# Layer 1's input projection: the second parts of two column tiles in one run, and two moved steps

## The chip, the cores and the metric

One core of a Trainium2 chip runs the whole kernel. The metric is the device time of one execution in microseconds; the median of three runs is taken. TensorE (PE) multiplies, VectorE (DVE) and ScalarE (ACT) work element by element, GpSimd (POOL) adds a few tiles and issues small DMAs, and SyncE (SP) issues the loads of weights.

## The reference, cut

Two layers over 256 tokens of width 2048, all in float32. Layer 1, the one that is changed, is a Mamba-2 layer:

```python
proj = x @ w_in
z, xbc, dt = jnp.split(proj, [SSD_D_INNER, SSD_D_INNER + SSD_CONV_DIM], -1)
xbc = jax.nn.silu(causal_depthwise_conv(xbc, conv_w, conv_b))
xs, bm, cm = jnp.split(xbc, [SSD_D_INNER, SSD_D_INNER + SSD_N_GROUPS * SSD_D_STATE], -1)
...
y = ssd_chunked(xs, dt, a, bm, cm, chunk)
y = y + d_skip.reshape(g, r)[..., None] * xs
yg = (y * jax.nn.silu(z.astype(jnp.float32))).reshape(b, L, g, SSD_NORM_GROUP)
yg = yg * lax.rsqrt(jnp.mean(yg * yg, -1, keepdims=True) + RMS_EPS)
yg = yg.reshape(b, L, SSD_D_INNER) * norm_g
return yg.astype(x.dtype) @ w_out
```

Layer 2 is sparse attention over the same tokens; the change does not touch it.

## The kernel before

**Split products.** A float32 product is made of three products of rounded parts: every operand is split into a first part, hi, and a second part, lo, and hi x hi + hi x lo + lo x hi are added up in PSUM. xT holds the hi and lo of x side by side, 512 columns per row tile. So with the weights' hi as the stationary operand, one matmul of 512 columns (L327) does hi x hi and hi x lo, and with the weights' lo one matmul of 256 columns (L324) does the third product.

**Units and the stream.** All weights go through one stream of units of 128 x 1024 elements (the class `Stream`). A unit is loaded by SP (L93) into one of four raw buffers, ScalarE copies it rounded into hi (L109), and VectorE subtracts to get lo (L138); hi and lo have four buffers each. `run` (L152) goes from unit to unit: it first has the units up to `i + SPLIT` (four) converted, then writes TensorE's matmuls of unit i, and then takes each side step under way one step on. That gives every engine its order; there is no scheduler, each engine works through its own list and waits by semaphores.

**The projection.** Layer 1's input projection has 160 units, numbered 0 to 159: 8 groups of 20, each group 10 column tiles of two units (one tile B, one C, four x, four z). `stream_w` (L306) writes a unit. For a column tile the order is hi of the first unit, lo of the first, lo of the second, hi of the second: a run of 16 lo matmuls, and, with the next tile's first unit, a run of 16 hi.

**Side steps.** When a column tile is finished, a generator (`conv_steps`, `z_steps`) evacuates it and works on it, a bit per unit. More generators start at unit numbers given by hand in the loop over groups (u = 20 g): `cb_steps` (the products of B and C, after unit u + 9), `xst_steps` (four transposes, the "turned rows" pxs, for the halves of a group, after u + 13 and u + 18), `m_steps` (the masks E and M), `y_steps` (after u + 23 and u + 33), which ends six units on with a matmul ms (L481) that sums the squares, and `norm_steps` for each two groups. A norm begins 40 units after the second group's start, waits for its small DMAs through POOL's queue, and then takes one tile in two units, eight tiles in all: VectorE multiplies (L516, into yf), ScalarE copies hi of yg, VectorE subtracts for its lo (L509). The output projection (`out_proj`, units 160 to 287) reads yg: units 160 to 171 read yg's first 24 tiles, two each.

Of the kernel before, what the change touches and what calls it, by code (L numbers as in the profile page):

```python
# [16 lines left out]
P = 128  # L17
T = 256
D = 2048
KT = D // P  # L20
NG = 8
# [27 lines left out]
SPLIT = 4  # L49
# [10 lines left out]
MOVING, FIRST8, OTHERS = range(3)  # L60


class Unit:


    def __init__(self, src, width, pe, use):
        self.src, self.width, self.pe, self.use = src, width, pe, use


class Stream:  # L70
# [7 lines left out]
        self.limit = 1 << 30  # L78
        self.homes = {}

    def add(self, src, width, pe, use):
        self.units.append(Unit(src, width, pe, use))
        return len(self.units) - 1

    def side(self, i, gen, behind=False):
# [66 lines left out]
    def run(self, end):  # L152
        while self.pos < end:
            i = self.pos
            self.convert_to(i + SPLIT)
            self.units[i].pe(*self.parts.pop(i))
            for behind, (fn, *a) in self.starts.pop(i, []):
                (self.behind if behind else self.active).append(fn(*a))
            self.active = [g for g in self.active if next(g, self) is not self]
            self.behind = [g for g in self.behind if next(g, self) is not self]  # L160
            self.pos += 1
# [9 lines left out]
def trunk_kernel(ctx: ExitStack, tc: tile.TileContext, x, xt, w1, wdt, dtp, prm, wo1,  # L171
                 wkv, wcq, wix, wg, wab, wo2, lnr, out):
    nc = tc.nc
# [12 lines left out]
    st = Stream(nc, wraw, whi, wlo)  # L186
    v = nc.vector

    def acc_tile(name):
        return p_acc.tile([P, 512], F32, tag="acc", name=name)  # L190
# [11 lines left out]
    xT = big.tile([P, KT, 2 * T], F32R, tag="A", name="xT")  # L202
# [20 lines left out]
    def rsqrt(pool, dst, val, n, w, tag):  # L223

        t = pool.tile([n, w], F32, tag=tag, name=tag)
        v.tensor_scalar(dst.bitcast(I32), val.bitcast(I32), -0.5, MAGIC, op0=ALU.mult,
                        op1=ALU.add)
        for k in range(3):
            v.tensor_mul(t, dst, dst)
            v.scalar_tensor_tensor(t, t, -0.5, val, op0=ALU.mult, op1=ALU.mult)  # L230
            v.scalar_tensor_tensor(dst, t, 1.5, dst, op0=ALU.add, op1=ALU.mult)
# [78 lines left out]
    def stream_w(half, cell, name, turn=True):  # L310


        def pe(h, l):
            if half == 0:
                cell["ps"] = acc_tile(name)
            ps, xs = cell["ps"], cell["x"][0]
            first, second = (1, 0) if half and turn else (0, 1)
            for lo in (first, second):
                for k in (0, 1, 6, 7, 4, 5, 2, 3) if lo and half == 0 else range(8):
                    kt, w = half * 8 + k, slice(k * P, (k + 1) * P)  # L320
                    last = half == 1 and lo == second and k == 7
                    if lo:
                        lw = l[:, w] if half else l[:, k // 2, k % 2 * P:(k % 2 + 1) * P]
                        nc.tensor.matmul(ps[:, 0:T], lw, xs[:, kt, 0:T], start=False,  # L324
                                         stop=last, skip_group_check=True)
                    else:
                        nc.tensor.matmul(ps, h[:, w], xs[:, kt, :], start=(kt == 0), stop=last,  # L327
                                         skip_group_check=True)
        return pe

    def halves(dst, ps, wait=True):
# [152 lines left out]
    def norm_steps(b):  # L484

        ms = sp1.tile([2, T], F32, tag="ms", name=f"msv{b}")
        nc.scalar.activation(ms, MS[b][0:2, 0:T], AF.Copy)
        md, rd = (dram.tile([2, T], F32, tag=t, name=f"{t}{b}") for t in ("ms_d", "rs_d"))
        nc.gpsimd.dma_start(md, ms)
        col = sp1.tile([P, 4], F32, tag="col", name=f"col{b}")  # L490
        rcl = sp1.tile([P, 4], F32, tag="rcl", name=f"rcl{b}")
        nc.gpsimd.dma_start(col, md.rearrange("g (q j) -> (g q) j", j=4))
        yield
        yield
        yield
        v.tensor_scalar_add(col, col, 4.0 * RMS_EPS)
        rsqrt(sp1, rcl, col, P, 4, "rq")
        nc.gpsimd.dma_start(rd.rearrange("g (q j) -> (g q) j", j=4), rcl)
        rb = sp1.tile([P, 2, T], F32, tag="rb", name=f"rbs{b}")
        nc.gpsimd.dma_start(rb, rd.rearrange("(o g) t -> o g t", o=1).broadcast_to([P, 2, T]))  # L500
        yield
        yield
        yield
        fts = {}
        for c in range(10):
            if c > 1:
                cc = 8 * b + c - 2
                dst = yg[cc // 16][:, cc % 16, :]
                v.tensor_sub(dst[:, T:2 * T], fts.pop(c - 2), dst[:, 0:T].bitcast(F32))  # L509
            if 0 < c < 9:  # L510
                cc = 8 * b + c - 1
                nc.scalar.activation(yg[cc // 16][:, cc % 16, 0:T], fts[c - 1], AF.Copy)
            if c < 8:
                g, cc = 2 * b + c // 4, 8 * b + c
                ft = fts[c] = sp3.tile([P, T], F32, tag="yf", name=f"yf{cc}")
                v.scalar_tensor_tensor(ft, G[g].pop(("x", c % 4)),  # L516
                                       par[:, PC_NORM + cc:PC_NORM + cc + 1],
                                       rb[:, c // 4, :], op0=ALU.mult, op1=ALU.mult)
            yield
            if b < 3:  # L520
                yield

    xcell = [xT]
    for g in range(NG):
        for kind, n in (("B", 1), ("C", 1), ("x", 4), ("z", 4)):
            for ci in range(n):
                cell = {"x": xcell}
                for half in range(2):
                    k = len(st.units)
                    i = st.add(w1[k], 1024, stream_w(half, cell, f"acc{k}", turn=k > 1),  # L530
                               OTHERS if half else FIRST8)
                if kind == "z":
                    st.side(i, (z_steps, g, ci, cell))
                else:
                    cc = {"x": g * 4 + ci, "B": 32 + g, "C": 40 + g}[kind]
                    st.side(i, (conv_steps, g, kind, ci, cc, cell))
# [67 lines left out]
    for g in range(NG):  # L604
        u = 20 * g
        gap = 5 if g < 7 else 2
        st.side(u + 9, (cb_steps, g))
        st.side(u + 13, (xst_steps, g, 0))
        st.side(u + 18 + (g == NG - 1), (xst_steps, g, 1))
        for c in range(4):  # L610
            st.side(max(u + 5 + gap * c, 9 + c), (abc_steps, g, c))
            st.side(u + 13 + gap * c, (m_steps, g, c))
            if c % 2:
                st.side(u + 18 + max(gap * c, 2 * c), (y_steps, g, c // 2))
        if g % 2:
            st.side(u + 18 + gap * 3 + 7, (norm_steps, g // 2), behind=g < NG - 1)
# [33 lines left out]
    for kt in range(KT):  # L650

        for h in range(2):
            nc.tensor.matmul(p_dt[h * NH1:(h + 1) * NH1, 0:P], w_dt[:, kt, :],
                             xr[:, kt, h * P:(h + 1) * P], start=(kt == 0),
                             stop=(kt == KT - 1), skip_group_check=True)
# [75 lines left out]
    def add_gate(h):  # L731
        cell = {"x": xcell}
        for half in range(2):
            i = st.add(wg[h * 2 + half], 1024, stream_w(half, cell, f"g{h}"),
                       OTHERS if half else FIRST8)
        st.side(i, (gate_steps, h, cell))
# [58 lines left out]
    for kb in range(8):  # L795
        i = st.add(wcq[kb], 1024, stream_tok(kb, 512, cells["q"], "qp",
                                             held if kb < EARLY else None), MOVING)
    st.side(i, (lat_norm, cells["q"], 512, PC_QG, 4, "q", "cqT"))
    for kb in range(8):
        i = st.add(wkv[kb], 672, stream_tok(kb, 336, cells["kv"], "kvp"), MOVING)  # L800
# [7 lines left out]
    def idx_pe(q, cell):  # L808
        def pe(h, l):
            cell["ps"] = acc_tile(f"ix{q}")  # L810
            for k in range(2):
                ps = cell["ps"][:, k * T:(k + 1) * T]
                for kt in range(4):
                    o = (k * 4 + kt) * P
                    nc.tensor.matmul(ps, h[:, o:o + P], cqT[:, kt, 0:T], start=(kt == 0), stop=False)
                    nc.tensor.matmul(ps, h[:, o:o + P], cqT[:, kt, T:2 * T], start=False, stop=False)
                    nc.tensor.matmul(ps, l[:, o:o + P], cqT[:, kt, 0:T], start=False, stop=(kt == 3))
        return pe
# [41 lines left out]
    for q in range(4):  # L860
        cell = {}
        i = st.add(wix[q], 1024, idx_pe(q, cell), MOVING)
# [130 lines left out]
    for p in range(NH2 // 2):  # L993
        src = wab[2 * p]
        i = st.add(wab[2 * p], 1024, pair_a(p), MOVING)
        st.side(i, (evac_steps, p, ("k", "v")))
        i = st.add(wab[2 * p + 1], 1024, pair_b(p), MOVING)
# [348 lines left out]
```

## Time and profile before

| | us |
|---|---|
| median of 3 runs (1230.06 to 1230.5) | 1230.15 |
| the profiled execution, its own time | 1230.57 |
| its span from first to last instruction | 1228.7 |
| TensorE busy in the span | 1223.0 |
| VectorE busy | 936.0 |
| ScalarE busy | 701.9 |
| end of layer 1's input projection (start of the output projection's first matmul, from the span's start) | 491.38 |

The span is what the trace covers; the time of an execution has a little more around it. TensorE's busy time counts matmuls that overlap in the engine's pipeline, so a full row there says only that it had work at hand; how fast it went is read from the distance of starts.

### The profile page before, as it was taken

The numbers are of one execution on the slowest core, as the hardware profiler recorded it, in microseconds if no ns is written. First come the engines' busy times: TensorE is split into PE (matmuls) and PEld (weight loads), VectorE is DVE, ScalarE is ACT, GpSimd is POOL, SyncE is SP. The second block draws the span as 40 slices with busy tenths as digits, with TensorE's granted clock in tenths as the row PEclk, the third lists the DMA queues.
The fourth block names the chain that finished last, engine by engine and source line by source line (L and its number), as shares of the span: only waits on it lengthen the run. The fifth ranks groups of instructions, "written<-read, shape, count | busy, mean of one in ns | idle before, by whom it ended". The sixth has DMA issues, their size and how long they took to land.

```text
span 1228.7 us, 19505 instructions
## 1 busy us (share of the span) xinstructions
PE 1223.0 (100%) x7197; PEld 1064.0 (87%) x7197; DVE 936.0 (76%) x1757; ACT 701.9 (57%) x1274; POOL 65.5 (5%) x102
## 2 busy tenths in 40 slices
PE   9999999999999999999999999999999999999998
PEld 8888888888888888788888898999999999888886
DVE  6978788988898889756557778877777777667457
ACT  6666566666666666544336655566766666433441
POOL 0001011001100110110000000000000000000000
PEclk9999999999999999999999999999999999999999
DMA  8765667566666665676666564454444445875652
GB/s 296 211 196 180 207 185 215 171 208 187 203 185 206 187 205 180 192 236 220 197 194 201 193 212 148 168 170 165 159 154 149 161 155 190 308 230 186 200 196 94
DMA packets 65359, 236.55 MB, mean 193 GB/s; under 512 B 8025, under 2 KB 8161, under 8 KB 64881
## 3 DMA queue, kind: packets, MB, share of 16 engines
q1 hardware_dynamic: 60352, 215.29, 54.2%
q0 software_dynamic: 4912, 20.02, 5.3%
q8 instruction: 57, 0.93, 0.3%
q14 instruction: 38, 0.30, 0.1%
HBM read 231.00 MB, written 4.28 MB: 191 GB/s over the span
## 4 chain that ended last, share of the span: by engine, by line
PE 99%; DMA 1%; SPq 0%; DVE 0%; ACT 0%; DVEq 0%; issue 0%
PE acc L327 24%; PE acc L324 12%; PE g L327 10%; PE o L555 9%; PE o L557 9%; PE o L556 9%; PE g L324 5%; PE y L452 2%; PE q L901 1%; PE q L900 1%; PE q L902 1%; PE pt L963 1%; PE pxs L432 1%; PE k L878 1%; PE k L879 1%; PE k L880 1%
## 5 line engine op out<-in xcount | busy, mean ns | idle before, releaser
L138 DVE TENSOR_TENSOR lo<-raw,hi 128x1024 fp32r<-128x1024 f32 (+1 forms) x404 | 489.0, 1214 | 240.2 <-ACT hi L109 239.8
L109 ACT ACTIVATE hi<-raw 128x1024 fp32r<-128x1024 f32 (+2 forms) x405 | 422.0, 1048 | 214.2 <-PE o L557 160.2
L327 PE MATMUL acc<-xT,hi 128*128 128x512 f32 x1280 | 314.5, 394 | 0.3 <-ACT hi L109 0.3
L327 PEld LDWEIGHTS acc<-xT,hi 128*128 128x128 f32 x1280 | 232.6, 188 | 46.3 <-ACT E L407 1.2
L324 PEld LDWEIGHTS acc<-xT,lo 128*128 128x128 f32 x1280 | 159.4, 188 | 6.4
L324 PE MATMUL acc<-xT,lo 128*128 128x256 f32 x1280 | 161.9, 278 | 0.0
L327 PE MATMUL g<-x1T,hi 128*128 128x512 f32 x512 | 127.4, 395 | 0.0
L327 PEld LDWEIGHTS g<-x1T,hi 128*128 128x128 f32 x512 | 92.4, 188 | 17.5
L555 PE MATMUL o<-hi,yg 128*128 128x512 f32 x256 | 100.3, 392 | 0.0
L557 PE MATMUL o<-hi,yg 128*128 128x512 f32 x256 | 99.7, 389 | 0.0
L556 PE MATMUL o<-lo,yg 128*128 128x512 f32 x256 | 99.6, 389 | 0.0
L555 PE MATMUL o<-hi,og 128*128 128x512 f32 (+1 forms) x256 | 99.6, 389 | 0.0
L557 PE MATMUL o<-hi,og 128*128 128x512 f32 (+1 forms) x256 | 98.9, 386 | 0.0
L556 PE MATMUL o<-lo,og 128*128 128x512 f32 (+1 forms) x256 | 98.8, 386 | 0.0
L354 DVE SCALAR_TENSOR_TENSOR ca<-cr,par,ca 128x255 f32<-128x255 f32 x144 | 69.2, 481 | 3.4
L324 PE MATMUL g<-x1T,lo 128*128 128x256 f32 x512 | 69.3, 280 | 0.0
L324 PEld LDWEIGHTS g<-x1T,lo 128*128 128x128 f32 x512 | 65.8, 188 | 2.9
L357 ACT ACTIVATE cr<-ca 128x256 f32<-128x256 f32 x48 | 20.1, 418 | 77.9 <-DVE ca L354 77.9
L555 PEld LDWEIGHTS o<-hi,yg 128*128 128x128 f32 x256 | 48.1, 188 | 10.1 <-issue 0.2
L557 PEld LDWEIGHTS o<-hi,yg 128*128 128x128 f32 x256 | 48.0, 188 | 10.1
L557 PEld LDWEIGHTS o<-hi,og 128*128 128x128 f32 x256 | 48.1, 188 | 9.9
L556 PEld LDWEIGHTS o<-lo,yg 128*128 128x128 f32 x256 | 48.1, 188 | 9.9
(274 smaller groups left out, 1781.8 us busy)
## 6 DMA issues: line engine op xcount, KB each, us to landing
raw<-in_w_dram SPq DMA_DIRECT2D x160, 512.0 KB, 4.2
raw<-in_wo_dram SPq DMA_DIRECT2D x128, 512.0 KB, 4.2
raw<-in_wg_dram SPq DMA_DIRECT2D x64, 512.0 KB, 3.2
raw<-in_wab_dram SPq DMA_DIRECT2D x32, 512.0 KB, 3.2
abc<-acs_d POOLq DMA_DIRECT2D x32, 256.0 KB, 4.2
raw<-in_wcq_dram SPq DMA_DIRECT2D x8, 512.0 KB, 4.4
raw<-in_wkv_dram SPq DMA_DIRECT2D x8, 336.0 KB, 2.9
scr<-in_xt_dram SPq DMA_DIRECT2D x4, 512.0 KB, 6.5
```

The source lines that it names most:

```text
L109: self.nc.scalar.activation(h[:, cs], r[:, cs], AF.Copy)
L138: eng.tensor_sub(*self.halfway.pop(i))
L324: nc.tensor.matmul(ps[:, 0:T], lw, xs[:, kt, 0:T], start=False, stop=last, skip_group_check=True)
L327: nc.tensor.matmul(ps, h[:, w], xs[:, kt, :], start=(kt == 0), stop=last, skip_group_check=True)
L354: v.scalar_tensor_tensor(acc[:, d:], rw[:, :T - d], w(k), acc[:, d:], op0=ALU.mult, op1=ALU.add)
L357: nc.scalar.activation(rw, acc, AF.Tanh)
L432: nc.tensor.transpose(pm[:, o:o + P], G[g][("x", 2 * half + c)][:, s * P:(s + 1) * P], ident)
L452: nc.tensor.matmul(py[ks, c * T + s * P:(c + 1) * T], xsT[:, s, c, ks], ms[c][k][:, ws], start=(c == 0 and s == 0), stop=(s == 1), skip_gr ...
L555: nc.tensor.matmul(ps, ah, hs, start=(kk == 2 * first), stop=False)
L556: nc.tensor.matmul(ps, ah, ls, start=False, stop=False)
L557: nc.tensor.matmul(ps, al, hs, start=False, stop=(kk == 31))
L878: nc.tensor.matmul(ps, h[:, o:o + P], ckvT[:, ct, 0:T], start=(ct == 0), stop=False)
```

## The change

Of the 160 units, those with `k % 20` up to 15, without the first four, are now taken in fours, that is, two column tiles a and b at a time, by a new function `stream_two`. Its order is: hi of a (two units), the first single hi matmul of b, lo of a (two units), lo of b (two units), and the rest of b's hi. The lo of a pair's first unit is thus used while the second unit is written, and `run` converts one unit less ahead at that step (`kept`). The last four units of a group, and the first four of all, keep the old order.

In `norm_steps` of the first three norms, a pause after the fourth of eight tiles moves the last four tiles five units later (four in the third norm). And `xst_steps` of a group's second half starts after u + 19 in all groups, not u + 18; the ms matmul of the group before stands after the same unit.

```diff
@@ -152,7 +153,7 @@
-            self.convert_to(i + SPLIT)
+            self.convert_to(i + SPLIT - (i > 0 and self.units[i - 1].kept))
@@ -328,6 +329,45 @@
+    def stream_two(j, a, b, name):
+        def hi(cell, half, h, ks):
+            for k in ks:
+                kt = half * 8 + k
+                nc.tensor.matmul(cell["ps"], h[:, k * P:(k + 1) * P], cell["x"][0][:, kt, :],
+                                 start=(kt == 0), stop=(cell is b and kt == 15),
+                                 skip_group_check=True)
+
+        def lo(cell, half, l):
+            for k in range(8) if len(l.shape) == 2 else (0, 1, 6, 7, 4, 5, 2, 3):
+                kt = half * 8 + k
+                lw = (l[:, k * P:(k + 1) * P] if len(l.shape) == 2 else
+                      l[:, k // 2, k % 2 * P:(k % 2 + 1) * P])
+                nc.tensor.matmul(cell["ps"][:, 0:T], lw, cell["x"][0][:, kt, 0:T], start=False,
+                                 stop=(cell is a and kt == 15), skip_group_check=True)
+
+        def pe(h, l):
+            after = st.parts.get(st.pos + 1)
+            if j == 0:
+                a["ps"] = acc_tile(name)
+                hi(a, 0, h, range(8))
+                a["lo"] = l
+            elif j == 1:
+                hi(a, 1, h, range(8))
+                b["ps"] = acc_tile(name + "b")
+                hi(b, 0, after[0], range(1))
+                lo(a, 0, a.pop("lo"))
+                lo(a, 1, l)
+            elif j == 2:
+                lo(b, 0, l)
+                lo(b, 1, after[1])
+                hi(b, 0, h, range(1, 8))
+            else:
+                hi(b, 1, h, range(8))
+        return pe
+
@@ -518,17 +558,26 @@
             if b < 3:
-                yield
+                for _ in range((6, 6, 5)[b] if c == 3 else 1):
+                    yield
...
+                if len(st.units) % 4 == 0:
+                    pair = [{"x": xcell} for _ in range(2)]
                 for half in range(2):
                     k = len(st.units)
-                    i = st.add(w1[k], 1024, stream_w(half, cell, f"acc{k}", turn=k > 1),
-                               OTHERS if half else FIRST8)
+                    if k < 4 or k % 20 > 15:
+                        i = st.add(w1[k], 1024, stream_w(half, cell, f"acc{k}", turn=k > 1),
+                                   OTHERS if half else FIRST8)
+                    else:
+                        cell = pair[k % 4 // 2]
+                        i = st.add(w1[k], 1024, stream_two(k % 4, *pair, f"acc{k}"),
+                                   OTHERS if k % 4 else FIRST8, kept=k % 4 == 0)
@@ -606,7 +655,7 @@
-        st.side(u + 18 + (g == NG - 1), (xst_steps, g, 1))
+        st.side(u + 19, (xst_steps, g, 1))
```

What this does to the orders of the engines is shown at four places. In the names, the number before the underscore counts units for hi, lo and raw, and tiles elsewhere; the one behind it counts buffers.

TensorE, units 68 to 71 (a pair, with the products cb of group 3), before:

```order
L327 MATMUL acc68_2409<-xT_86,hi68_2307 128x512 x8
L324 MATMUL acc68_2409<-xT_86,lo68_2308 128x256 x8
L324 MATMUL acc68_2409<-xT_86,lo69_2345 128x256 x8
L327 MATMUL acc68_2409<-xT_86,hi69_2344 128x512 x8
L381 MATMUL cb3_2470<-C3_2426,B3_2367 128x256
L382 MATMUL cb3_2470<-C3_2426,B3_2367 128x128
L327 MATMUL acc70_2479<-xT_86,hi70_2376 128x512 x8
L324 MATMUL acc70_2479<-xT_86,lo70_2377 128x256 x8
L324 MATMUL acc70_2479<-xT_86,lo71_2404 128x256 x8
L327 MATMUL acc70_2479<-xT_86,hi71_2403 128x512 x8
```

The same units on TensorE now:

```order
L339 MATMUL acc68_2409<-xT_86,hi68_2340 128x512 x8
L339 MATMUL acc68_2409<-xT_86,hi69_2346 128x512 x8
L339 MATMUL acc69b_2441<-xT_86,hi70_2384 128x512
L348 MATMUL acc68_2409<-xT_86,lo68_2341 128x256 x8
L348 MATMUL acc68_2409<-xT_86,lo69_2347 128x256 x8
L421 MATMUL cb3_2466<-C3_2418,B3_2375 128x256
L422 MATMUL cb3_2466<-C3_2418,B3_2375 128x128
L348 MATMUL acc69b_2441<-xT_86,lo70_2385 128x256 x8
L348 MATMUL acc69b_2441<-xT_86,lo71_2404 128x256 x8
L339 MATMUL acc69b_2441<-xT_86,hi70_2384 128x512 x7
L339 MATMUL acc69b_2441<-xT_86,hi71_2403 128x512 x8
```

The two runs of 16 lo matmuls are one of 32, and cb has moved from between hi matmuls into the middle of it.

TensorE, units 78 to 80 (the last tile of group 3 and the next group's first unit; pxs3_1 are the turned rows, ms1 the squares), before:

```order
L324 MATMUL acc78_2763<-xT_86,lo78_2662 128x256 x8
L432 MATMUL pxs3_1_2783<-ident_90,xs3_2_2644 128x128 x2
L432 MATMUL pxs3_1_2783<-ident_90,xs3_3_2721 128x128 x2
L324 MATMUL acc78_2763<-xT_86,lo79_2699 128x256 x8
L327 MATMUL acc78_2763<-xT_86,hi79_2698 128x512 x8
L481 MATMUL ms1_2820<-sq2_3_2687,sel_99 128x256
L327 MATMUL acc80_2835<-xT_86,hi80_2731 128x512 x8
```

The same units on TensorE now:

```order
L325 MATMUL acc78_2755<-xT_86,lo78_2666 128x256 x8
L325 MATMUL acc78_2755<-xT_86,lo79_2695 128x256 x8
L328 MATMUL acc78_2755<-xT_86,hi79_2694 128x512 x8
L521 MATMUL ms1_2802<-sq2_3_2683,sel_99 128x256
L472 MATMUL pxs3_1_2811<-ident_90,xs3_2_2652 128x128 x2
L472 MATMUL pxs3_1_2811<-ident_90,xs3_3_2717 128x128 x2
L339 MATMUL acc80_2826<-xT_86,hi80_2723 128x512 x8
```

The transposes stand behind ms, and no longer inside the lo run.

VectorE, around the steps of units 64 to 66 (xs2 is y's evacuation, M are masks, B3 is group 3's B), before:

```order
L459 SCALAR_TENSOR_TENSOR xs2_1_1879<-xs2_1_1879,par_88,y2_0_2244 128x256
L461 TENSOR_TENSOR xs2_1_1879<-xs2_1_1879,zs2_1_2001 128x256
L138 TENSOR_TENSOR lo68_2308<-raw68_2170,hi68_2307 128x4x256
L420 TENSOR_TENSOR M20_2335<-E20_2253,cbm2_1825 128x384
L420 TENSOR_TENSOR M21_2337<-E21_2256,cbm2_1825 128x384
L138 TENSOR_TENSOR lo69_2345<-raw69_2197,hi69_2344 128x1024
L363 SCALAR_TENSOR_TENSOR B3_2367<-cr35_2191,ca35_2190 128x256
```

The same place on VectorE now:

```order
L499 SCALAR_TENSOR_TENSOR xs2_1_1871<-xs2_1_1871,par_88,y2_0_2244 128x256
L501 TENSOR_TENSOR xs2_1_1871<-xs2_1_1871,zs2_1_2001 128x256
L460 TENSOR_TENSOR M20_2331<-E20_2253,cbm2_1833 128x384
L460 TENSOR_TENSOR M21_2333<-E21_2256,cbm2_1833 128x384
L139 TENSOR_TENSOR lo68_2341<-raw68_2193,hi68_2340 128x4x256
L139 TENSOR_TENSOR lo69_2347<-raw69_2199,hi69_2346 128x1024
L403 SCALAR_TENSOR_TENSOR B3_2375<-cr35_2187,ca35_2186 128x256
```

The conversion of a pair's first unit stands a step later, with that of the second. From B3 on to C3, the other operand of cb, VectorE's rows are the same in both.

VectorE, where the third norm ends (yf22 and yf23 are its last two tiles), before:

```order
L509 TENSOR_TENSOR yg1_563<-yf22_5532,yg1_563 128x256
L138 TENSOR_TENSOR lo166_5668<-raw166_5538,hi166_5667 128x1024
L138 TENSOR_TENSOR lo167_5687<-raw167_5582,hi167_5686 128x1024
L509 TENSOR_TENSOR yg1_563<-yf23_5614,yg1_563 128x256
L138 TENSOR_TENSOR lo168_5715<-raw168_5620,hi168_5714 128x1024
```

And now:

```order
L549 TENSOR_TENSOR yg1_563<-yf22_5659,yg1_563 128x256
L139 TENSOR_TENSOR lo170_5758<-raw170_5665,hi170_5757 128x1024
L139 TENSOR_TENSOR lo171_5778<-raw171_5684,hi171_5777 128x1024
L549 TENSOR_TENSOR yg1_563<-yf23_5709,yg1_563 128x256
L139 TENSOR_TENSOR lo172_5797<-raw172_5715,hi172_5796 128x1024
```

Both tiles stand four conversions later.

## Rows read from the trace of the kernel before

**Rows 1.** The page's chain that ended last, by engine.

```profile
PE 99%; DMA 1%; SPq 0%; DVE 0%; ACT 0%; DVEq 0%; issue 0%
```

**Rows 2.** Waits of TensorE, whole run: engine, line, for whom; us, times, longest.

```profile
PE p_dt L631 <- DVE scr L628: 1.3, 1, 1.3
PE acc L327 <- ACT hi L109: 0.3, 1, 0.3
```

**Rows 3.** Timeline of TensorE: start us, us to last end, operation, shapes, number.

```profile
222.06 2.00 PE L324 MATMUL acc<-xT,lo 128*128 128x256 f32 x16
223.90 3.81 PE L327 MATMUL acc<-xT,hi 128*128 128x512 f32 x16
227.55 2.00 PE L324 MATMUL acc<-xT,lo 128*128 128x256 f32 x16
```

**Rows 4.** The same runs, from windows that begin at their second parts.

```profile
222.99 1.07 PE L324 MATMUL acc<-xT,lo 128*128 128x256 f32 x8
...
225.51 2.20 PE L327 MATMUL acc<-xT,hi 128*128 128x512 f32 x9
```

**Rows 5.** TensorE in the output projection: window, us, busy (number), clock, DMA.

```profile
563.33:576.93 13.60, 13.60 (x61) 1.00 0.58 167
```

**Rows 6.** Timeline of TensorE: pxs in a lo run, ms in a hi run.

```profile
426.70 1.09 PE L324 MATMUL acc<-xT,lo 128*128 128x256 f32 x8
427.64 0.60 PE L432 MATMUL pxs<-ident,xs 128*128 128x128 f32 x4
...
428.99 2.00 PE L327 MATMUL acc<-xT,hi 128*128 128x512 f32 x8
430.83 0.59 PE L481 MATMUL ms<-sq,sel 128*128 128x256 f32 x2
...
433.12 2.01 PE L324 MATMUL acc<-xT,lo 128*128 128x256 f32 x16
```

**Rows 7.** Timeline of TensorE, group 7's end: ms and pxs together.

```profile
488.75 2.00 PE L327 MATMUL acc<-xT,hi 128*128 128x512 f32 x8
...
491.02 0.60 PE L432 MATMUL pxs<-ident,xs 128*128 128x128 f32 x4
491.38 0.47 PE L555 MATMUL o<-hi,yg 128*128 128x512 f32 x1
...
494.00 0.39 PE L557 MATMUL o<-hi,yg 128*128 128x512 f32 x1
```

**Rows 8.** Timeline of TensorE: cb, then y with pxs, between hi matmuls.

```profile
398.37 2.00 PE L327 MATMUL acc<-xT,hi 128*128 128x512 f32 x8
...
402.70 0.63 PE L324 MATMUL acc<-xT,lo 128*128 128x256 f32 x4
...
410.02 2.00 PE L327 MATMUL acc<-xT,hi 128*128 128x512 f32 x8
411.96 1.52 PE L452 MATMUL y<-M,xsT 128*64 128x256 f32 x16
...
415.73 0.52 PE L324 MATMUL acc<-xT,lo 128*128 128x256 f32 x3
```

**Rows 9.** Timelines of VectorE and TensorE: a tile's last writer and its reader.

```profile
217.36 0.42 DVE L363 SCALAR_TENSOR_TENSOR C<-cr,ca 128x256 f32<-128x256 f32 x1
...
219.57 0.59 PE L381 MATMUL cb<-C,B 128*128 128x256 f32 x2
...
243.57 1.22 DVE L138 TENSOR_TENSOR lo<-raw,hi 128x1024 fp32r<-128x1024 f32 x1
...
247.35 1.05 PE L324 MATMUL acc<-xT,lo 128*128 128x256 f32 x7
...
276.76 1.22 DVE L138 TENSOR_TENSOR lo<-raw,hi 128x1024 fp32r<-128x1024 f32 x1 [0.79 <-ACT hi L109]
...
282.28 2.00 PE L324 MATMUL acc<-xT,lo 128*128 128x256 f32 x16
```

**Rows 10.** VectorE: a 40 us window over all engines; its timeline in the output projection.

```profile
200.00:240.00 40.00, 40.00 (x245) 34.04 (x245) 36.95 (x78) 26.03 (x51) 4.33 (x7) 1.00 0.63 196
...
512.46 1.23 DVE L138 TENSOR_TENSOR lo<-raw,hi 128x1024 fp32r<-128x1024 f32 x1 [1.39 <-ACT hi L109]
```

More of the change, by code (lines that the diff above doesn't have):

```diff
@@ L63, with __init__ @@
 class Unit:
-    def __init__(self, src, width, pe, use):
-        self.src, self.width, self.pe, self.use = src, width, pe, use
+    def __init__(self, src, width, pe, use, kept):
+        self.src, self.width, self.pe, self.use, self.kept = src, width, pe, use, kept
 class Stream:
@@ L79, in __init__, with add @@
         self.homes = {}
-    def add(self, src, width, pe, use):
-        self.units.append(Unit(src, width, pe, use))
+    def add(self, src, width, pe, use, kept=False):
+        self.units.append(Unit(src, width, pe, use, kept))
         return len(self.units) - 1
@@ L520, in norm_steps @@
             if b < 3:
-                yield
-    xcell = [xT]
+                for _ in range((6, 6, 5)[b] if c == 3 else 1):
+                    yield
+    xcell, pair = [xT], None
     for g in range(NG):
```

## The prediction, made before the changed kernel was run

> **What bounds the kernel now.** I read the chain that ended last first: 99% of it is TensorE [rows 1]. Then TensorE's waits over the whole run: two, of 1.3 and 0.3 us [rows 2]. So through layer 1's input projection (160 units of weights, up to about 491 us) TensorE hardly ever waits; whatever changes the time must either change what the matmuls themselves take in a row, or make a wait where there is none. The granted clock is 1.00, the 2.4 GHz level, throughout.
>
> Next the timeline of TensorE, row by row. A column tile's matmuls stand as 16 lo (256 columns) and 16 hi (512 columns): from 222.06 to 223.90 and from 223.90 to 227.55 [rows 3]. Is that the plain rate? A long row of equal 512-column matmuls, in the output projection, gives it: 60 starts in 13.60 us (61 are counted, one was in flight), 0.2267 us each, and a 256-column matmul at half of that 0.1133 us [rows 5]. By these rates 16 of each are 3.627 + 1.813 = 5.44 us; the rows give 227.55 - 222.06 = 5.49. Cutting the runs shows where the rest sits: the first eight lo matmuls take 222.99 - 222.06 = 0.93 us and the second eight 223.90 - 222.99 = 0.91; the first seven hi matmuls take 225.51 - 223.90 = 1.61 us against 7 x 0.2267 = 1.59, the last nine 227.55 - 225.51 = 2.04, which is the plain rate [rows 3, 4]. So each change of width costs about 0.02 us, in the handful of matmuls behind it, and one lo run inside a hi run costs 0.02 + 0.023 = 0.043 by the halves, 0.05 by the whole. I take 0.046.
>
> **Part 1, one lo run for two column tiles.** Of the 160 units, those with number modulo 20 up to 15, without the first four, form 31 pairs of tiles (4 in each of 8 groups, less one). Before, a pair has two lo runs of 16; now it has one of 32, behind a single hi matmul of the second tile, which the order rows show. No matmul is added or taken away. Saved: 31 x 0.046 = 1.43 us. The bounds: 0 if the longer run gives back at its end or in its middle what it saves, and 31 x 0.093 = 2.9 us if the remaining switch cost nothing either. The rows are of the same two widths in the same tiles, so I take the value between.
>
> The rows give 0.02 us more for the first eight lo matmuls than for the second eight [rows 3, 4]. A rule speaks against part 1: the Trainium skill, "TensorE: Matmul & The Clock Gate", section "Back-to-back issue gap", prices a warm matmul by its columns alone (columns at 2.4 GHz and 2.5 ns), whatever stood before it; by that regrouping is worth nothing. The trace does not agree with that price: it has 0.2267 us where the page's figures give an estimated 0.216.
>
> **Part 2, the turned rows with the squares.** Before, the four transposes pxs of a group's second half stand inside a lo run, and the ms matmul one unit later inside a hi run. The first costs 428.99 - 426.70 = 2.29 us against 1.84 for a clean lo run, 0.45; the second 433.12 - 428.99 = 4.13 against 3.65, 0.48, and the lo run behind it is 0.01 longer [rows 3, 6]. Group 7 has them side by side already: 488.75 to 494.00 is 5.25 us for 8 + 11 hi matmuls, ms and pxs; 19 x 0.2267 and 0.02 for the switch are 4.33, so the two together cost 0.92 [rows 7]. Side by side saves 0.45 + 0.48 + 0.01 - 0.92 = 0.02; groups 1 to 6 gain it: 6 x 0.02 = 0.1 us. Group 0 has no ms there and is unchanged within that size.
>
> **Part 3, what now interrupts a lo run.** cb (after unit 9 of a group) and y with pxs (after unit 13) stood between two hi matmuls and now stand in the middle of the run of 32. In hi runs cb costs 402.70 - 398.37 - 3.65 = 0.68 us and y with pxs 415.73 - 410.02 - 3.65 = 2.06 [rows 8]; most of that is their own work. In lo runs the trace shows only pxs alone, 0.45 for four transposes. Between hi matmuls, the eight in front of y take 411.96 - 410.02 = 1.94 where eight behind a switch take 1.84, so 0.1 us is lost at that edge, and in a lo run this may be as much, nothing, or more. Bounds: 0.04 either way for the 8 cb and 0.1 either way for the 8 y with pxs, together 1.1 us either way. I take 0: the rest of the cost is the fp32 matmuls themselves, which do not change.
>
> **Part 4, the norm's last four tiles.** No instruction is added. In the three norms that run under the projection VectorE and ScalarE do the same four tiles five blocks later (four for the third). TensorE waits for neither before, so this gains nothing by itself; it relieves VectorE just where its lead over TensorE is smallest: the lo of unit 79 ends at 243.57 + 1.22 = 244.79 and TensorE starts on it at 247.35, a lead of 2.6 us [rows 9]. The cost is a later yg. In the third norm the last yg tile now stands behind lo of unit 171, at step 168, and its first reader is unit 171 of the output projection, three units of 12 x 0.2267 = 2.72 us later. There VectorE is idle 1.39 us in each unit, waiting for ScalarE [rows 10], so the tile is done within a unit of its place: covered. The x tiles that the norm reads are free, by the count of steps, about ten units before a convolution takes them again.
>
> **Part 5, the conversions.** The lo part of a pair's first unit is kept through the second, so the step after it converts nothing and the next converts two (order rows of VectorE). What was needed earlier? In a pair, hi of the second and third unit is needed 1.8 us earlier (the 16 lo matmuls of the first tile, 16 x 0.1133, stand behind them now), lo of the third and fourth 1.6 us earlier (7 hi matmuls of 0.2267 stand behind them now). The lead that I can read: lo of unit 91, a fourth unit, ends at 277.98; its lo run starts at 282.28, and the unit's own eight 0.93 later, at 283.21: 5.2 us [rows 9]. Less 1.6 and less one more lo in front of it (1.22) leaves 2.4 us. Shortest of all is the lead of C: it ends at 217.78, cb starts at 219.57, 1.8 us [rows 9]. The order of VectorE between B and C is the same as before, cb stands 0.23 us later (one hi matmul in front of the lo run), so this lead stays. VectorE is busy 36.95 of 40 us in its fullest stretch [rows 10], so it does catch up, slowly. SP's loads follow each conversion by a step, as before, so at most they go out one unit later, and in twos; POOL's queue keeps its order save for the moved steps. Each conversion that is late holds up TensorE and all that stands behind it there. Cost taken: 0. If that cover is gone, see the third rival.
>
> **Sum.** -1.43 - 0.1 = -1.5 us. The profiled execution took 1230.57 us (span 1228.7 and 1.9 around it); it would take 1229.0. It stands 0.42 above the median of the three runs, 1230.15, from which the sum gives 1228.6.
>
> **Rivals.**
> First, no saving: the loss is not of the switch but of something that returns elsewhere in the longer run (part 1 gives 0). For: I see only its size, not its cause. Against: it recurs at each switch alike. Time 1230.15 - 0.1 = 1230.0. (The rule of the Trainium skill named in part 1 would end there too.)
> Second, a larger gain: the edge of y that costs 0.1 us between hi matmuls shrinks between lo matmuls, and cb's by 0.04, so part 3 gives 1.1. For: pxs in a lo run costs only 0.45, and the last lo in front of it shows almost no loss. Against: y's weights have another width than its neighbours in both places. Time 1228.6 - 1.1 = 1227.5.
> Third, slower: VectorE's lead ends. The mechanism is lo of a pair's fourth unit, needed 1.6 us earlier and converted behind a double. It decides from a lag 2.4 us larger than in the stretch of unit 91; unit 79's shorter lead (2.6 us against 5.2) shows that a norm can bring such a lag. If the moved norm tiles meet the pairs of the next group so, a wait of some 1 us in each of the two groups that each of three norms touches is 6 us: 1234.6. It is slower than before from 1.5 us of such waits on. Against: the total work of VectorE is unchanged, and units 78 and 79 keep their old order.
>
> **How the numbers follow.** Forecast 0.58, no saving 0.14, larger gain 0.14, VectorE's lead 0.14 (0.08 of it over 1232.6). A measurement of this kernel tells about 0.2%, 2.46 us, from no change: faster means under 1227.7. The larger gain and a little of the forecast's lower edge lie there: 0.16. Slower: 0.08. Within: 0.76. The range takes in the first rival and its rounding, up to 1230.6, and the larger gain to 1227.2; left out are most of the third rival and gains beyond part 3's bound.
>
> **What would show it.** Right: TensorE's timeline has lo runs of 32 from start to next hi in about 32 x 0.1133 + 0.02 = 3.65 us; a pair without interruption takes 10.93 us instead of 10.98; TensorE still has only the two waits; the output projection starts about 1.5 us earlier than 491.38. Wrong on part 1: the second half of the 32 is slower than 0.1133 each. Wrong on part 3: a lo run with cb or with y and pxs exceeds a clean one by other than 0.68 and 2.06. Wrong on part 5: TensorE's waits list VectorE's lo or C, and the projection ends later than before.

## The result and the profile after

The changed kernel takes 1236.53 us (median of 6 runs, 1235.83 to 1237.34) against 1230.18 us before: a ratio of 1.0053, 95% interval 1.0043 to 1.0063. It is slower by 6.35 us; 1228.6 was forecast, with a range up to 1230.6.

The chain that ended last is no longer TensorE's alone (against [rows 1]):

```profile
PE 81%; DVE 12%; ACT 4%; issue 2%; DMA 1%; DVEq 0%; SPq 0%; ACTq 0%
```

TensorE's waits over the whole run (engine, line, for whom; us in total, times, longest), where before there were two ([rows 2]):

```profile
PE acc L325 <- DVE lo L139: 3.3, 5, 1.1
PE p_dt L680 <- DVE scr L677: 1.3, 1, 1.3
PE acc L328 <- ACT hi L110: 0.4, 1, 0.4
PE cb L421 <- DVE C L403: 0.3, 2, 0.2
PE acc93b L339 <- DVE cr L375: 0.2, 1, 0.2
```

The first, fourth and fifth are new, and all three wait for VectorE. The output projection starts at 497.23, 5.85 us later than the 491.38 before (TensorE's timeline: start us, us, operation):

```profile
497.23 0.47 PE L604 MATMUL o<-hi,yg 128*128 128x512 f32 x1
```

And yet the runs themselves are what the forecast said. TensorE's timeline of a pair that nothing interrupts, units 20 to 23:

```profile
73.47 2.00 PE L348 MATMUL acc<-xT,lo 128*128 128x256 f32 x16
75.31 1.98 PE L348 MATMUL acc21b<-xT,lo 128*128 128x256 f32 x16
77.12 3.59 PE L339 MATMUL acc21b<-xT,hi 128*128 128x512 f32 x15
```

The 32 lo matmuls take 77.12 - 73.47 = 3.65 us, the forecast number: 1.84 for the first sixteen, as in [rows 3], and 1.81, the plain rate, for the rest. So the saving exists, and something larger was lost on top. The place where it is lost is read from the same view at units 78 and 79, where a group ends:

```profile
245.35 1.09 PE L325 MATMUL acc<-xT,lo 128*128 128x256 f32 x8
247.15 1.20 PE L325 MATMUL acc<-xT,lo 128*128 128x256 f32 x8 [0.71 <-DVE lo L139]
248.19 1.09 PE L328 MATMUL acc<-xT,hi 128*128 128x512 f32 x4
```

Sixteen lo matmuls take 2.84 us instead of 1.84: TensorE stands before the second eight until VectorE has written lo of unit 79. The idle time shown, 0.71, is less than the 1.0 us lost. The first eight are listed as busy for 1.09 us, where the first eight of a clean run take 0.93 [rows 3, 4], so 0.16 of the wait counts as busy; and the second eight take 248.19 - 247.15 = 1.04 instead of 0.91, 0.13 more.

Now the engine that is waited for. VectorE's and ScalarE's longest waits from 20 to 490 us, first before, then after:

```profile
DVE lo L138 <- ACT hi L109: 53.4, 53, 2.7
...
ACT cr L357 <- DVE ca L354: 77.9, 48, 3.3
```

```profile
DVE lo L139 <- ACT hi L110: 63.4, 61, 2.3
...
ACT cr L397 <- DVE ca L394: 108.2, 48, 4.2
```

VectorE's work is the same (935.2 us busy against 936.0), but it waits 10 us longer for hi from ScalarE, and ScalarE waits 30 us longer, at the tanh of a convolution (cr from ca), for VectorE. The two hold each other up. ScalarE's timeline shows how, first before, around the conversion of unit 76:

```profile
228.31 0.41 ACT L512 ACTIVATE yg<-yf 128x256 fp32r<-128x256 f32 x1
228.61 1.05 ACT L109 ACTIVATE hi<-raw 128x1024 fp32r<-128x1024 f32 x1
231.88 0.42 ACT L357 ACTIVATE cr<-ca 128x256 f32<-128x256 f32 x1 [2.21 <-DVE ca L354]
```

hi of unit 76 is made at 228.61, and then ScalarE waits 2.21 us for the convolution's sum. After, ScalarE and below it VectorE:

```profile
230.16 0.41 ACT L552 ACTIVATE yg<-yf 128x256 fp32r<-128x256 f32 x1
233.73 0.42 ACT L397 ACTIVATE cr<-ca 128x256 f32<-128x256 f32 x1 [3.16 <-DVE ca L394]
...
235.50 2.00 ACT L110 ACTIVATE hi<-raw 128x1024 fp32r<-128x1024 f32 x2
...
236.57 2.36 DVE L139 TENSOR_TENSOR lo<-raw,hi 128x1024 fp32r<-128x1024 f32 x2 [1.42 <-ACT hi L110]
```

hi of unit 76 now stands behind that tanh, with hi of unit 77. ScalarE waits 3.16 us with nothing to do and makes both only at 235.50, though by the trace the load of unit 76 had landed at 227.72. VectorE has come to lo of unit 76 in its order and stands still for 1.42 us until the first hi is there. That is theory A.

### The profile page after: what moved, and what is told of

Its sections match the earlier page's. It is cut to its first block, busy times and chain, and to the rows that moved or that the text cites. A ratio compares the mean times of both kernels' runs of the same rounds, so it can differ in the third digit from the quotient of the medians.

```text
span 1234.6 us, 19489 instructions
## 1 busy us (share of the span) xinstructions
PE 1224.7 (99%) x7197; PEld 1064.7 (86%) x7197; DVE 935.2 (76%) x1757; ACT 697.5 (56%) x1274; POOL 66.0 (5%) x102
## 4 chain that ended last, share of the span: by engine, by line
PE 81%; DVE 12%; ACT 4%; issue 2%; DMA 1%; DVEq 0%; SPq 0%; ACTq 0%
PE g L328 10%; PE o L604 9%; PE o L606 9%; PE o L605 9%; PE g L325 5%; PE acc L339 5%; DVE lo L139 5%; PE acc L328 4%; DVE ca L394 3%; PE acc L348 2%; PE acc L325 2%; ACT hi L110 2%; PE q L950 1%; PE q L949 1%; PE q L951 1%
## 5 line engine op out<-in xcount | busy, mean ns | idle before, releaser
L339 PE MATMUL acc<-xT,hi 128*128 128x512 f32 x496 | 119.2, 392 | 0.0
L339 PEld LDWEIGHTS acc<-xT,hi 128*128 128x128 f32 x496 | 92.0, 188 | 19.9 <-issue 0.7
L328 PE MATMUL acc<-xT,hi 128*128 128x512 f32 x288 | 70.6, 391 | 0.4 <-ACT hi L110 0.4
L348 PEld LDWEIGHTS acc<-xT,lo 128*128 128x128 f32 x496 | 61.6, 188 | 2.2
L328 PEld LDWEIGHTS acc<-xT,hi 128*128 128x128 f32 x288 | 52.6, 188 | 11.1 <-ACT hi L110 0.8
L348 PE MATMUL acc<-xT,lo 128*128 128x256 f32 x496 | 62.1, 278 | 0.0
```

Source lines behind the costliest of these rows:

```text
L339: nc.tensor.matmul(cell["ps"], h[:, k * P:(k + 1) * P], cell["x"][0][:, kt, :], start=(kt == 0), stop=(cell is b and kt == 15), skip_group ...
L348: nc.tensor.matmul(cell["ps"][:, 0:T], lw, cell["x"][0][:, kt, 0:T], start=False, stop=(cell is a and kt == 15), skip_group_check=True)
```

## The experiments

Three theories were put against each other. **A:** the deferred conversion has a ScalarE half, hi, which moved behind a tanh that waits for VectorE; VectorE idles for it and falls behind. **B:** TensorE's new order asks for the lo parts 1.6 us earlier, and that alone ends VectorE's lead (the forecast's third rival). **C:** the norm's last four tiles meet other work in their new place.

**e1_hi_early: the changed kernel, one conversion's hi back at its old step.**

```diff
-            self.convert_to(i + SPLIT - (i > 0 and self.units[i - 1].kept))
+            kept = i > 0 and self.units[i - 1].kept
+            self.convert_to(i + SPLIT - kept)
+            if kept and self.ready < self.limit:
+                k = self.ready
+                h = self.early[k] = self.whi.tile([P, 1024], F32R, tag="hi", name=f"hi{k}")
+                self.nc.scalar.activation(h, self.raws[k], AF.Copy)
```

(and the conversion itself then takes that hi.)

> The changed kernel, but ScalarE makes hi of the deferred unit at the old step, ahead of the tanh that waits for VectorE; only VectorE's lo of it stays a step later. Theory A (hi now stands behind that tanh, VectorE then idles for hi and falls behind): VectorE's waits on hi in the projection go back from 63 to about 53 us, TensorE's waits for lo vanish, 1228.5 to 1230.0 us. Theory B (TensorE asks for the lo parts 1.6 us earlier, whatever ScalarE does): about 1236, waits stay. Theory C (the norm's last four tiles meet other work now): about 1236.

Measured: 1228.72 us against 1229.89 of the kernel before in the same session, ratio 0.999 (0.9981 to 0.9999). TensorE's waits, VectorE's waits from 20 to 490 us, ScalarE's timeline at unit 76, and the start of the output projection:

```profile
PE p_dt L690 <- DVE scr L687: 1.3, 1, 1.3
...
DVE lo L144 <- ACT hi L113: 49.6, 61, 2.0
...
228.71 1.04 ACT L166 ACTIVATE hi<-raw 128x1024 fp32r<-128x1024 f32 x1
231.97 0.42 ACT L407 ACTIVATE cr<-ca 128x256 f32<-128x256 f32 x1 [2.22 <-DVE ca L404]
...
489.83 0.47 PE L614 MATMUL o<-hi,yg 128*128 128x512 f32 x1
```

The whole loss is gone, with the new order of TensorE, the doubled lo on VectorE, the norm and the turned rows all in place. The output projection starts 491.38 - 489.83 = 1.55 us earlier than before, and 1.5 was the forecast; but part of that is luck. The last lo run that is the same in both kernels, that of units 2 and 3, stands here (before, then e1):

```profile
20.27 2.00 PE L324 MATMUL acc<-xT,lo 128*128 128x256 f32 x16
...
19.93 2.00 PE L335 MATMUL acc<-xT,lo 128*128 128x256 f32 x16
```

So 0.34 us of the 1.55 had been gained before the first pair, where TensorE has the same order in both; in the ten traces this row starts anywhere from 19.21 to 20.27. From it to the output projection the kernel before takes 491.38 - 20.27 = 471.11 us, e1 489.83 - 19.93 = 469.90 and the changed kernel 477.26. The saving is 1.2 us, as in the medians (1229.89 - 1228.72 = 1.17), and the loss on top of it 7.4.

Run by run, e1 and the changed kernel have the same runs of matmuls in the same order, and the sum of what each takes longer in the changed kernel is these 7.4 us: 4.8 at the lo of a group's last unit (five groups, 0.67 to 1.43), 1.6 in five hi runs at the second tile's first matmul, and 1.0 at cb in two groups. The profile puts two of the five hi waits down to the evacuation of an older tile (cr); for the other three it names no releaser. None of it lies before 221 us: in the first three groups the leads are just long enough (0.3 us at units 39 and 59), and from the fourth on, where the first norm runs, they are not.

**e3_bunch: the kernel before, with the conversions alone put off.**

```diff
-            self.convert_to(i + SPLIT)
+            kept = 4 < i < 160 and i % 4 == 1 and i % 20 < 16
+            self.convert_to(i + SPLIT - kept)
```

> The kernel before, with the conversions alone put off as in the changed kernel: none at the second unit of each four, two at the third; TensorE's order, norm and turned rows as before. Theory A: the delay is there without the new order: VectorE's waits on hi rise by about 10 us, TensorE waits for lo of each group's last unit, 1235 to 1238 us. Theory B: 1230.2, no waits. Theory C: 1230.2, no waits.

Measured: 1237.35 us against 1229.89, ratio 1.0059 (1.0046 to 1.0071). TensorE's waits, VectorE's from 20 to 497 us, and ScalarE around unit 76:

```profile
PE pxs L433 <- DVE xs L364: 2.0, 2, 1.0
PE acc L325 <- DVE lo L138: 1.8, 3, 1.3
...
DVE lo L138 <- ACT hi L109: 63.3, 56, 2.3
...
234.25 0.42 ACT L358 ACTIVATE cr<-ca 128x256 f32<-128x256 f32 x1 [3.17 <-DVE ca L355]
...
236.02 1.99 ACT L109 ACTIVATE hi<-raw 128x1024 fp32r<-128x1024 f32 x2
```

The loss is there, 7.5 us, without the new order, without the norm's move and without the turned rows' move. As e1 has all of these and no loss, theories B and C fall as causes of it. TensorE waits at pxs here too, which in this kernel still stands a unit earlier.

**e6_bunch_hi_early: e3 with hi back at its old step.** The edit is e1's, on e3. TensorE and VectorE have the same orders in both.

> The kernel before with the conversions put off as in e3_bunch, but hi of the deferred unit made by ScalarE at the old step; VectorE and TensorE have the same order as in e3_bunch. Theory A (the place of that one hi in ScalarE's order is the whole loss): 1229.6 to 1230.6 us, no waits of TensorE beyond the first 20 us, VectorE's waits on hi below 55 us. Rival B2 (the doubled lo on VectorE costs as well): 1232 to 1236, TensorE waits for lo of a group's last units.

Measured: 1230.17 us against 1230.08, ratio 1.0002 (0.9993 to 1.0011). VectorE's waits and ScalarE at unit 76:

```profile
DVE lo L143 <- ACT hi L112: 52.9, 53, 2.7
...
228.16 1.05 ACT L165 ACTIVATE hi<-raw 128x1024 fp32r<-128x1024 f32 x1
231.43 0.42 ACT L367 ACTIVATE cr<-ca 128x256 f32<-128x256 f32 x1 [2.21 <-DVE ca L364]
```

So the doubled lo on VectorE costs nothing that shows: from the lo run of units 2 and 3 to the output projection e6 takes 471.11 us, as the kernel before. The place of one hi per four units in ScalarE's order is the whole 7.2 us between e3 and e6. Theory A is shown, by both pairs: e3 and e6, and the changed kernel and e1.

**e4_norm_old and e5_norm_new: the norm's move taken back, and alone.**

```diff
-                for _ in range((6, 6, 5)[b] if c == 3 else 1):
-                    yield
+                yield
```

> The changed kernel with the norm's last four tiles where they were before. Theory A: the delay stays and the norm's tiles add to it just before each group's last unit: 1237 to 1241 us. Theory B: about 1236.5. Theory C: back to 1228.5 to 1229.5.

> The kernel before with the norm's last four tiles five blocks later and nothing else. Theory A and B: 1230.2 within 0.3, the lead of unit 79's lo over TensorE longer than 2.6 us. Theory C: 1234 to 1237, waits of TensorE.

Measured: e4 1235.64 us against 1229.89, ratio 1.0046 (1.0033 to 1.0059); e5 1229.79, ratio 0.9999 (0.999 to 1.0008). The move alone changes no time; the lead of unit 79's lo (TensorE's start on it less its end on VectorE) is 3.3 us in e5, longer than 2.6, as expected. Theory A's number for e4, 1237 to 1241, was too high: without the move the changed kernel is not worse but about as slow as with it, so the move does not shorten TensorE's waits. Theory C falls by both.

**e7_hi_norm_old: e1 with the norm in its old place.** The edit is e4's, on e1.

> e1_hi_early with the norm's last four tiles back in their old place. If the move of the norm covers something once the conversions are in order: TensorE waits for lo of units 79, 119 or 159, 1229 to 1231 us. If it covers nothing: 1228.7 within 0.4, with the lead of unit 159's lo near 1 us.

Measured: 1228.83 us against 1230.08, ratio 0.9991 (0.9982 to 1.0). The lead of unit 159's lo over TensorE is 1.4 us in e1 and 0.75 here, that of unit 79's 1.9 and 1.2; but at unit 99, in the next group, it is 1.8 in e1 and 2.8 here. The move buys 0.7 us of lead in the groups where a norm begins, takes 1.0 us in the groups that its last tiles now reach, and gains no time.

**e8_hi_first8: another place in memory for the lo behind y and pxs.**

```diff
-                                   OTHERS if k % 4 else FIRST8, kept=k % 4 == 0)
+                                   OTHERS if k % 4 and k % 20 != 14 else FIRST8, kept=k % 4 == 0)
```

> e1_hi_early; lo of the unit that follows y and pxs (number modulo 20 is 14) lies and is read as the first eight of a lo run. If its slow matmuls of 0.118 us come from how that lo lies: they end within its eight and each of seven places saves 0.05 to 0.1 us, 1228.1 to 1228.6 in all. If they come from the interruption itself: 1228.7, and they stay.

Measured: 1228.84 us against 1230.08, ratio 0.9991 (0.9982 to 1.0). The sixteen lo matmuls behind y and pxs take 1.97 us in e8 as in e1: laid out as for the first eight of a run it is as slow. What makes the difference to cb stays open.

**e9_all_pairs: e1 with every column tile in a pair.**

```diff
-                    if k < 4 or k % 20 > 15:
+                    if k < 4:
```

> e1_hi_early with all ten tiles of a group, and the first ones, in pairs. By the switch's price 9 lo runs fewer save 9 x 0.046 = 0.4 us: 1228.3. But a group's last unit is now the fourth of a pair, whose lo is asked for 1.6 us earlier, and its lead in e1_hi_early is 1.4 to 1.9 us where a norm runs: if the advance of theory B is real, TensorE waits there in five groups for up to 0.5 us each, and the saving is gone: 1228.5 to 1230.5.

The edit reaches the last four units of each group; the first four of all stay as they were, so eight lo runs are saved and not nine. Measured: 1228.94 us against 1230.08, ratio 0.9991 (0.9982 to 1.0), not to be told from e1. In its trace only the last group's pair loses (TensorE's timeline, units 156 to 159):

```profile
480.89 2.00 PE L358 MATMUL acc<-xT,lo 128*128 128x256 f32 x16
482.72 2.37 PE L358 MATMUL acc157b<-xT,lo 128*128 128x256 f32 x16
484.93 0.86 PE L349 MATMUL acc157b<-xT,hi 128*128 128x512 f32 x3
```

4.04 us instead of 3.65. In the other groups the earlier need was covered, though the leads in e1 (1.4 to 1.9 us in the groups with a norm) were near the advance of 1.6; 0.16 to 0.24 us of lead is left there. The 0.39 us lost in the last pair is about what eight switches save, 8 x 0.046 = 0.37: from the lo run of units 2 and 3 to the output projection e9 takes 469.93 us, e1 469.90. Here theory B's advance does cost something, in one place.

e1, e7, e8 and e9 cannot be told apart; all four are 0.1% under the kernel before, with intervals that end at 0.9999 or 1.0, and by the medians e1 is 7.8 us under the changed kernel.

## Why the prediction was wrong

**What bounds the kernel: right.** TensorE without waits, and any gain only from the matmuls' own row.

**Part 1, the price of a switch: right.** A run of 32 takes 3.65 us. A pair that nothing interrupts begins here, and the next pair's lo run at 97.00 (first row of the timeline under part 3):

```profile
86.07 2.00 PE L348 MATMUL acc<-xT,lo 128*128 128x256 f32 x16
```

That is 10.93 us, where two tiles took 2 x 5.49 = 10.98 before [rows 3], as forecast. The price by columns alone, the rule of the Trainium skill that was weighed there ("TensorE: Matmul & The Clock Gate", section "Back-to-back issue gap", which states it for an isolated matmul), would have put e1 at the time before, less 0.1. The interval of e1 just excludes no change, and the pairs in the traces say it plainly.

The whole gain was a little smaller than forecast: 1.2 us in e1 instead of 1.5, and what is missing is in part 3. That e1's projection starts 1.55 us earlier, and that its time of 1228.72 lies so near the forecast 1228.6, is luck: the sum went out from 1230.15, and in e1's session the kernel before took 1229.89.

**Part 2: not shown by the time.** In e1, as in group 7 before, ms and pxs stand together; the term was 0.1 us of the 1.5 and cannot be told apart in the time.

**Part 3: a small loss where 0 was taken.** TensorE's timeline of the changed kernel, at cb and at y with pxs in the middle of a lo run:

```profile
97.00 2.00 PE L348 MATMUL acc<-xT,lo 128*128 128x256 f32 x16
...
101.32 0.40 PE L339 MATMUL acc29b<-xT,hi 128*128 128x512 f32 x1
...
108.60 2.00 PE L348 MATMUL acc<-xT,lo 128*128 128x256 f32 x16
...
112.39 2.13 PE L348 MATMUL acc33b<-xT,lo 128*128 128x256 f32 x16
114.36 0.63 PE L339 MATMUL acc33b<-xT,hi 128*128 128x512 f32 x2
```

cb costs 101.32 - 97.00 - 3.65 = 0.67 us (0.68 in a hi run, [rows 8]), y with pxs 114.36 - 108.60 - 3.65 = 2.11 (2.06). In a lo run cb is 0.01 us cheaper and y with pxs 0.05 to 0.06 dearer. There are seven places of y with pxs, not eight (group 0 has no y there), so some 0.4 us is lost, inside the bounds that were given. The second rival, a larger gain, did not come.

**Part 4: right that it gains nothing by itself (e5), half right that it relieves VectorE.** The lead of unit 79's lo grows by 0.7 us (e5), but that of unit 99's shrinks by 1.0; where the lead was lost, the move did not help (e4). The shortest lead of a lo before was not that of unit 79 either, but that of unit 159, 1.8 us.

**Part 5, the conversions, is the step that failed.** "Cost taken: 0" was worked out from VectorE's order and from leads read on VectorE: one more lo in front, 1.22 us, and an advance of 1.6. That sum was sound: with hi back in place the lead of unit 91's lo is 2.5 us (e1), where 2.4 was worked out. But a conversion is two instructions on two engines. The deferral also moved hi on ScalarE, past every side step of a unit, and among them is the tanh, for which ScalarE already waited 77.9 us in total before. I read the order of TensorE and VectorE and not that of ScalarE, which was 57% busy (701.9 us of the span of 1228.7) and waited for by TensorE once, for 0.3 us [rows 2]. The term that was set to 0 measures 7.4 us; 7.4 less the 1.2 gained is the 477.26 - 471.11 = 6.15 by which the stage became longer, and the time rose by 6.35.

The third rival had the right engine and the right end, VectorE's lead, and nearly its price (1234.6). Its mechanism was wrong: not the earlier need (e3 has the loss without it) nor the doubled lo (e6 has that without the loss), and the places are not a pair's fourth unit but the last unit of a group, cb, and the second tile's first hi matmul. So the nearness of its price is luck. In hindsight its chance of 0.14 was too low: VectorE's shortest leads were 1.8 us, and VectorE, 92% busy in its fullest stretch, had little room to win back 10 us more of waiting.

Of ScalarE's order a rule was at hand: the Trainium skill, "TensorE: Matmul & The Clock Gate", in the table at its head, has the queues of ScalarE and VectorE as strict first in, first out. The trace agrees: in the changed kernel ScalarE stands idle for 3.16 us, up to the tanh at 233.73, while hi of unit 76, which e1 makes at 228.71, waits behind it.

## What to carry to other kernels

When a step is moved, go through its instructions one by one and read the order of each engine that has one, above all of an engine that is far from busy: an engine that works in order and waits for another is a place that nothing should be put behind. If engine X waits for Y and Y for X, a short instruction that moves behind X's wait makes both idle, and that eats the lead of a nearly full Y though no work was added. A lead is to be read at every place where the bound engine waits for Y, and the shortest one counts.

## What the runs showed of the hardware that was not expected

Behind y with pxs the lo matmuls do not settle. Sixteen take 114.36 - 112.39 = 1.97 us; the first has an edge of about 0.09, and the others stay near 0.118 us each, against 0.113 behind cb and in clean runs. The last ten of a run show it, in the changed kernel behind cb and then behind y with pxs:

```profile
100.19 1.30 PE L348 MATMUL acc29b<-xT,lo 128*128 128x256 f32 x10
...
113.18 1.34 PE L348 MATMUL acc33b<-xT,lo 128*128 128x256 f32 x10
```

They take 101.32 - 100.19 = 1.13 us and 114.36 - 113.18 = 1.18. This is about the 0.06 us a place that part 3 had at 0: 15 x 0.0045 = 0.07. In a lo run behind pxs alone they settled in the kernel before (its TensorE timeline, in the run of [rows 6]):

```profile
427.99 1.17 PE L324 MATMUL acc<-xT,lo 128*128 128x256 f32 x8
```

Eight take 428.99 - 427.99 = 1.00 us here, which is the edge of about 0.09 and eight at 0.113. The other layout of lo in memory (e8) does not change it. The cause is open.
